# A decoder layer in split float32: three products taken from 256 tokens as columns to 512 weight columns with the tokens on partitions

## The chip, the cores and the metric

One core of one Trainium2 chip runs the whole kernel. The metric is device microseconds of one execution; smaller is better. The kernel before took 768.17 us, the median of three runs (767.91 to 768.85).

## The reference, cut to what matters

One layer on 256 tokens of width 1024, all in float32: a feed-forward block, a mixer with two branches in parallel (a Mamba-2 state-space branch, "SSD", of inner width 2048, and a differential attention of 8 heads), and a second feed-forward block. The part around the change is this:

```
u = rmsnorm(h, mix_pre_g)
z, xbc, dt_raw, q, k, v, gate_logits = split(u @ w_in)          # gate_logits: 2 x 1024 columns
y_ssd = ssd_branch(...)     # ends in  y (256 x 2048) @ ssd_w_branch (2048 x 1024)
y_att = diff_attn_branch(...)   # ends in  o (256 x 1024) @ da_w_branch (1024 x 1024)
gates = sigmoid(gate_logits + gate_b).reshape(b, L, 2, D_MODEL)
merged = gates[:, :, 0] * y_ssd + gates[:, :, 1] * y_att
h = h + rmsnorm(merged @ w_out, mix_post_g)
```

In the attention each head has two score matrices; its weights are softmax(first) minus lambda times softmax(second), causal, with a linear position bias, and the output of each head is normalised over its 128 columns before da_w_branch.

## The kernel before, in words

**Three terms for each product.** TensorE is fed with fp32r, a rounded float32. So each operand is split in two, a high part (the rounded value) and a low part (what is left), and a product is the sum of three: high by high, low by high and high by low. Activations are split by `split` (L185), a cast on ScalarE (L186) and a subtraction on VectorE (L187); weights likewise when they have been loaded (L162 and L163).

**Weights.** They come in chunks of 1 MB, in the order in which they are used, on SP's DMA queue into three buffers (tag `raw`). `take` (L175) hands out the halves of the next chunk and sees to it that the splits of the chunks behind it have been issued, three chunks ahead (AHEAD). The splits, two high and two low tiles of 128 x 1024 for a chunk, and most other larger tiles share 29 buffers of 4 KB in each partition (tag `k4`).

**Two kinds of product.** `mm_t` (L189) makes a transposed result: the weight's 128 columns are the stationary operand, and the 256 tokens are the moving columns, so channels lie on partitions. A chunk of 1024 rows by 256 columns makes 2 blocks of 128 channels with 8 x 3 matmuls each, 48 in all. `mm_nat` (L218) makes a natural result: 128 tokens are the stationary operand, and 512 columns of weights move, so tokens lie on partitions. A chunk there is 512 rows by 512 columns and makes, for each of two blocks of tokens, 4 x 3 matmuls, 24 in all. Before the change, `mm_nat` makes only the V product and the first products of the feed-forward blocks (its matmul is L227).

**Order of the stages.** Feed-forward 1; the mixer's norm; V; dt, B, C and xs with the convolution; z; q and k; then the gates (8 chunks, L944 to L958, tile `pgt`), the SSD branch's product (8 chunks, L966 to L974, tile `pws`), the attention branch's product (4 chunks, L981 to L992, tile `pwd`), w_out (4 chunks, `mm_n`, L408), and feed-forward 2. `mm_n` takes the merged result with channels on partitions (it is its stationary operand there) and gives tokens on partitions. The gates' bias and the sigmoid are applied with channels on partitions: ScalarE adds the bias, one column for each 128 channels from a table of constants, as it empties PSUM. The two branches' results are multiplied by the gates on VectorE, in place in the gates' tiles, and the merged tile is split for w_out.

**Background work.** What lies between the large products is written as generators that are put in a queue and run piece by piece between the chunks: the products inside the SSD branch (`ssd_work`), its norm (`ssd_norm`), and the attention (`att_work`, L821). After each chunk `back.run(BG_US)` issues pieces worth 2.8 us of estimated time. A head of the attention issues: scores (PE, tile `psc`), mask and position bias (DVE), the maximum (DVE), four exponentials with their sums (ACT), the weighting by the sums and the difference (DVE), three transposes (PE, tile `pa`), a copy (ACT, tile `aT`) and two value products (PE, tile `po`). After every second head comes the norm of the pair: a square on ACT, a sum over partitions as a product with ones (PE, tile `pno`), a logarithm and an exponential (ACT), a multiplication (DVE) and a split. ScalarE's tables of functions are loaded explicitly (L234): one for exponentials and logarithms, one for the sigmoid, one for SiLU. Before the SSD branch's product, pieces are run until its input is there; after it, all that is left of the attention.

**The order on each engine.** In the first part of the program and in the tail of `mm_n` it is the order written (`own_order`). From the end of the mixer's first products on it is chosen by the scheduler of the language when the kernel is built (`free_order`), each engine having one queue that is worked in order.

**PSUM.** Three banks rotate for the large products (`pj`), five for everything else (`bg`). A bank has 512 float32 in each partition. In `mm_t` one bank holds both blocks of 128 channels.

Of the kernel before, what the change touches and what calls it, by code (L numbers as in the profile page):

```python
# [15 lines left out]
F32R = mybir.dt.float32r  # L16
AF = mybir.ActivationFunctionType
ALU = mybir.AluOpType
# [6 lines left out]
P = 128  # L25
T = 256
D = 1024
FF = 2816
KD = D // P
# [12 lines left out]
BG_US = 2.8  # L42
# [3 lines left out]
def tile_hybrid_layer(ctx: ExitStack, tc: tile.TileContext, x, ffn1_pre_g, ffn1_w_gate, ffn1_w_up,  # L46
# [4 lines left out]
    nc = tc.nc  # L51
# [5 lines left out]
    def k4(shape, name, dt=F32):  # L57
        return sb.tile(shape, dt, tag="k4", name=name, bufs=K4_BUFS)
# [13 lines left out]
    def pj(name):  # L72

        return ps.tile([P, 512], F32, tag="pj", name=name, bufs=3)

    def pjt(name):

        return pj(name).rearrange("p (m t) -> p m t", m=2)

    def bg(shape, name):  # L80
        return ps.tile(shape, F32, tag="bg", name=name, bufs=5)
# [4 lines left out]
    def t_chunk(w, k0, c0):  # L86
        chunks.append((w[k0:k0 + D, c0:c0 + T].rearrange("(j p) c -> p j c", p=P), [P, KD, T]))

    def s_chunk(w, k0, c0):
        chunks.append((w[k0:k0 + 512, c0:c0 + 512].rearrange("(j p) c -> p j c", p=P), [P, 4, 512]))  # L90
# [4 lines left out]
    w_in2 = w_in[0]  # L95
    Z0, XS0, B0, C0, DT0, Q0, KK0, V0, G0 = 0, 2048, 4096, 4608, 5120, 5152, 6176, 7200, 8224
# [21 lines left out]
    for c in range(4):  # L118
        t_chunk(w_in2, 0, Q0 + c * T)
        t_chunk(w_in2, 0, KK0 + c * T)  # L120
    for c in range(8):
        t_chunk(w_in2, 0, G0 + c * T)
    for c in range(4):
        t_chunk(ssd_w_branch[0], 0, c * T)
        t_chunk(ssd_w_branch[0], D, c * T)
    for c in range(4):
        t_chunk(da_w_branch[0], 0, c * T)
    for c in range(4):
        n_chunk(w_out[0], c * 2 * P)
    ffn_chunks(ffn2_w_gate, ffn2_w_up, ffn2_w_down)  # L130
# [38 lines left out]
    def split_to(n):  # L169

        while len(splits) < min(n, len(chunks)):
            for _ in split_steps():
                pass

    def take(ahead=AHEAD):  # L175

        i = taken[0]
        taken[0] += 1
        split_to(i + ahead)
        his, los = splits[i]  # L180
        splits[i] = None
        nj = chunks[i][1][1] // 2
        return (lambda j: his[j // nj][:, j % nj, :], lambda j: los[j // nj][:, j % nj, :])

    def split(hi, lo, src):  # L185
        nc.scalar.copy(hi, src)  # L186
        nc.vector.tensor_sub(lo, src, hi.bitcast(F32))  # L187

    def mm_t(acc, w, act, k0=0, first=True, last=True):  # L189

        (wh, wl), (ah, al, _) = w, act
        acc = acc if isinstance(acc, list) else [acc[:, m, :] for m in range(2)]
        for m in range(2):
            cs = slice(m * P, (m + 1) * P)
            for j in range(KD):
                nc.tensor.matmul(acc[m], wh(j)[:, cs], ah(k0 + j), start=first and j == 0, stop=False)  # L196
                nc.tensor.matmul(acc[m], wh(j)[:, cs], al(k0 + j), start=False, stop=False)  # L197
            for j in range(KD):
                nc.tensor.matmul(acc[m], wl(j)[:, cs], ah(k0 + j), start=False,  # L199
                                 stop=last and j == KD - 1)  # L200
# [17 lines left out]
    def mm_nat(acc, w, act, k0, first, last, late):  # L218


        (wh, wl), (ah, al) = w, act
        pairs = [(ah, wh), (al, wh), (ah, wl)] if late == "w" else [(ah, wh), (ah, wl), (al, wh)]
        terms = [(p, j) for j in range(4) for p in pairs[:2]] if late == "w" else \
            [(p, j) for p in pairs[:2] for j in range(4)]
        terms += [(pairs[2], j) for j in range(4)]
        for i, ((a, b), j) in enumerate(terms):
            nc.tensor.matmul(acc, a(k0 + j), b(j), start=first and i == 0, stop=last and i == 11)  # L227
# [5 lines left out]
    def act_table(name):  # L233
        f = nc.scalar.preload_act_table_set(name)  # L234
        for prev in act_since:
            tc.add_manual_dep(f.ins, prev, order, reason="activation table")
        act_since.clear()
        act_fence[0] = f.ins.name

    def act(*args, **kw):  # L240
        a = nc.scalar.activation(*args, **kw)
        if act_fence[0] is not None:
            tc.add_manual_dep(a.ins, act_fence[0], order, reason="activation table")
        act_since.append(a.ins.name)
# [19 lines left out]
    halves = (slice(0, 512), slice(512, D))  # L264
# [8 lines left out]
    ident = const.tile([P, P], F32, name="ident")  # L273
# [19 lines left out]
    pt = bg([P, KD], "pt_cols_f")  # L293
    nc.tensor.transpose(pt, stage_f, ident[:KD, :KD])
    nc.vector.tensor_copy(cols_f, pt)
    cols_a = const.tile([P, P], F32, name="cols_a")
    col, gain_rows = {}, []
    row = 0
    for name, v in (("mx", mix_pre_g), ("f2", ffn2_pre_g), ("gb", gate_b),
                    ("ng", ssd_norm_g), ("cb", ssd_conv_b), ("sg", da_subln_g)):  # L300
        n = v.shape[1] // P
        gain_rows.append((row, n, v))
        col[name] = row
        row += n
# [4 lines left out]
    def new_u(tag):  # L309
        for i in range(2):  # L310
            uT[i] = sb.tile([P, 4, 2, T], F32R, tag="u8", name=f"u{i}_{tag}", bufs=2)

    act_u = (lambda j: uT[j // 4][:, j % 4, 0, :], lambda j: uT[j // 4][:, j % 4, 1, :],
             lambda j: uT[j // 4][:, j % 4, :, :])
    uh, ul, _ = act_u
# [87 lines left out]
    def load_gain(v, name):  # L403
        pg = k4([P, D], name)
        nc.gpsimd.dma_start(pg, v[0].partition_broadcast(P))
        return pg
# [197 lines left out]
    pt = bg([P, P], "pt_cols_b")  # L604
# [13 lines left out]
    for o, n, off in ((0, P, 0), (P, T, P)):  # L618
        v = dneg[:, o:o + n]
# [110 lines left out]
    for i in range(4):  # L730
        acc = pjt(f"pbc{i}")
# [17 lines left out]
    yh = [None] * 4  # L749
    yl = [None] * 4  # L750
# [67 lines left out]
    oh = [None] * 2  # L818
    ol = [None] * 2
# [85 lines left out]
    back = Background()  # L905
    back.add(cb_work())
    for g in range(4):
        xs[g] = k4([P, 4, T], f"xs{g}")
        for i in range(2):
            acc = pjt(f"pxs{g}{i}")  # L910
# [5 lines left out]
    for g in range(4):  # L916
        sz[g] = k4([P, 4, T], f"sz{g}")
        for i in range(2):
            acc = pjt(f"pz{g}{i}")
# [8 lines left out]
    for c in range(4):  # L928
# [4 lines left out]
        acc = pjt(f"pq{c}")  # L933
# [3 lines left out]
        acc = pjt(f"pk{c}")  # L937
# [3 lines left out]

    back.add(att_work())

    def gates(half):  # L944
        tiles = []
        for c in range(4):
            if c % 2 == 0:
                tiles.append(k4([P, 4, T], f"gt{half}{c}"))
            acc = pjt(f"pgt{half}{c}")
            mm_t(acc, take(), act_u)  # L950
            for m in range(2):
                n = col["gb"] + half * 8 + c * 2 + m
                nc.scalar.activation(tiles[-1][:, (c % 2) * 2 + m, :], acc[:, m, :], AF.Identity,
                                     bias=cols_a[:, n:n + 1])
            back.run(BG_US)
        return tiles

    gt0, gt1 = gates(0), gates(1)  # L958
    act_table(SIGMOID)
    for t in gt0 + gt1:  # L960
        act(t, t, AF.Sigmoid)
    act_table(EXP_LN)
    while yl[3] is None:
        back.run(0.1)
    act_y = (lambda j: yh[j // 4][:, j % 4, :], lambda j: yl[j // 4][:, j % 4, :], None)
    for c in range(4):  # L966
        acc = [pj(f"pws{c}{m}")[:, :T] for m in range(2)]
        mm_t(acc, take(), act_y, 0, True, False)
        back.run(BG_US)
        mm_t(acc, take(), act_y, KD, False, True)  # L970
        for m in range(2):
            t = gt0[c // 2][:, (c % 2) * 2 + m, :]
            nc.vector.tensor_tensor(t, acc[m], t, ALU.mult)
        back.run(BG_US)  # L974
    del act_y
    yh = yl = None
    back.drain()
    act_table(SILU)
    act_o = (lambda j: oh[j // 4][:, j % 4, :], lambda j: ol[j // 4][:, j % 4, :], None)
    mg = []  # L980
    for c in range(4):  # L981
        acc = pjt(f"pwd{c}")
        mm_t(acc, take(), act_o)
        cs = slice((c % 2) * 2, (c % 2) * 2 + 2)
        t0, t1 = gt0[c // 2][:, cs, :], gt1[c // 2][:, cs, :]
        nc.vector.tensor_tensor(t1, acc, t1, ALU.mult)
        nc.vector.tensor_tensor(t1, t1, t0, ALU.add)
        if c % 2 == 0:
            mh = k4([P, 4, T], f"mh{c}", F32R)
            ml = k4([P, 4, T], f"ml{c}", F32R)  # L990
        split(mh[:, cs, :], ml[:, cs, :], t1)
        mg += [(mh[:, cs.start + m, :], ml[:, cs.start + m, :]) for m in range(2)]  # L992
    pg = load_gain(mix_post_g, "pg_mx")
    acc = [[bg([P, 512], f"acc_mx{b}{q}") for q in range(2)] for b in range(2)]

# [49 lines left out]
```

## Time and the profile before

| | us |
|---|---|
| three runs | 767.91, 768.17, 768.85 |
| profiled execution | 768.8 |
| its span | 766.0 |
| PE busy in it | 751.8 (98%) |
| DVE busy | 522.5 (68%) |
| ACT busy | 441.7 (58%) |
| POOL busy | 32.7 (4%) |
| gates, from first product to the first of the SSD branch | 411.70 to 468.70 |
| SSD branch | 468.70 to 529.00 |
| attention branch | 529.00 to 552.05 |
| w_out | 552.05 to 574.74 |
| feed-forward 2 to the end | 574.74 to 766.0 |

PE is TensorE's queue of matmuls, PEld its loads of stationary operands, DVE VectorE, ACT ScalarE, POOL GpSimd and SP the engine that issues most DMAs. In the timeline, a row gives the start and the duration in us, the engine, the line of the kernel, the operation with out<-in tiles, partitions x elements, and how many like it follow each other; in brackets stands the idle time of the engine before it with what ended it. In a table by stretches, the columns are the stretch, its length, busy time and number of instructions of PE, PEld, DVE, ACT and POOL, the granted clock of TensorE, the DMA engines' busy share, and GB/s. In a group of instructions the columns after the bar are busy time in us and mean duration in ns. Matmuls follow each other before the last has ended, so their durations overlap.

### The profile page before, as it was taken

What the parts mean: (1) busy time and instruction counts of PE and PEld (TensorE: products, weight loads), DVE (VectorE), ACT (ScalarE), POOL (GpSimd) and SP (SyncE); (2) the same over time, 40 slices, a digit from 0 to 9 for tenths busy, and PEclk for the clock granted to TensorE, in tenths of its full rate; (3) what the DMA queues carried; (4) which work ended last, traced back from release to release, by engine and by line L of the source; (5) the groups of instructions that cost most, each with busy time, mean ns of one, the idle gap of its engine ahead of it and who ended that gap; (6) DMA issues with size and microseconds to landing.
All of it is one profiled execution on the core that took longest, in us unless ns stands there. A gap on an engine that the chain in (4) does not pass through costs nothing.

```text
span 766.0 us, 11904 instructions
## 1 busy us (share of the span) xinstructions
PE 751.8 (98%) x4811; PEld 668.9 (87%) x4811; DVE 522.5 (68%) x815; ACT 441.7 (58%) x721; POOL 32.7 (4%) x73
## 2 busy tenths in 40 slices
PE   8899999999999999999999999999999999999996
PEld 6688888888889999899999988989988888888885
DVE  5586677654577888887868777676785767666612
ACT  7475566553566565666836767665573656555511
POOL 3300000000200000000000000000011000000000
PEclk9999999999999999999999999999999999999999
DMA  9576665586253638465535554436481676545801
GB/s 322 131 237 204 220 220 219 172 297 219 62 165 113 214 119 267 145 219 177 182 110 172 160 164 143 133 114 217 171 296 56 200 240 194 173 169 186 296 0 55
DMA packets 104199, 136.97 MB, mean 179 GB/s; under 512 B 2668, under 2 KB 88784, under 8 KB 104144
## 3 DMA queue, kind: packets, MB, share of 16 engines
q1 hardware_dynamic: 101728, 129.51, 51.4%
q0 software_dynamic: 2112, 6.18, 2.6%
q8 instruction: 37, 0.61, 0.3%
q10 hardware_dynamic: 304, 0.53, 0.2%
q14 instruction: 18, 0.15, 0.1%
HBM read 135.13 MB, written 1.08 MB: 178 GB/s over the span
## 4 chain that ended last, share of the span: by engine, by line
PE 88%; DVE 4%; ACT 3%; issue 1%; POOL 0%; DVEq 0%; POOLq 0%; ACTq 0%
PE acc_f L422 16%; PE pup_f L212 9%; PE pg_f L212 9%; PE pn_f L227 4%; PE pg_f L211 4%; PE pup_f L211 4%; PE pn_mx L227 3%; PE acc_mx L422 3%; PE pxs L197 2%; PE pxs L199 2%; PE pxs L196 2%; PE pz L196 2%; PE pz L199 2%; PE pz L197 2%; PE pgt L199 1%; PE pgt L196 1%
## 5 line engine op out<-in xcount | busy, mean ns | idle before, releaser
L163 DVE TENSOR_TENSOR wlo<-raw,whi 128x1024 fp32r<-128x1024 f32 (+1 forms) x246 | 291.2, 1211 | 47.5 <-ACT whi L162 47.1
L162 ACT CAST whi<-raw 128x1024 fp32r<-128x1024 f32 (+1 forms) x246 | 247.1, 1042 | 52.8 <-PE acc_f L422 18.4
L212 PE MATMUL pg_f<-u_f,whi 128*128 128x512 f32 x288 | 101.2, 396 | 0.0
L212 PE MATMUL pup_f<-u_f,whi 128*128 128x512 f32 x288 | 101.1, 396 | 0.0
L211 PE MATMUL pg_f<-u_f,wlo 128*128 128x256 f32 x252 | 70.6, 280 | 0.0
L211 PE MATMUL pup_f<-u_f,wlo 128*128 128x256 f32 x252 | 70.4, 279 | 0.0
L212 PEld LDWEIGHTS pg_f<-u_f,whi 128*128 128x128 f32 x288 | 53.0, 188 | 9.6
L212 PEld LDWEIGHTS pup_f<-u_f,whi 128*128 128x128 f32 x288 | 52.8, 188 | 9.7
L422 PE MATMUL acc_f<-whi,gh_f 128*128 128x512 f32 x176 | 58.2, 390 | 0.0
L422 PE MATMUL acc_f<-wlo,gh_f 128*128 128x512 f32 x176 | 58.2, 390 | 0.0
L422 PE MATMUL acc_f<-whi,gl_f 128*128 128x512 f32 x176 | 58.1, 389 | 0.0
L211 PEld LDWEIGHTS pup_f<-u_f,wlo 128*128 128x128 f32 x252 | 47.6, 189 | 1.6
L211 PEld LDWEIGHTS pg_f<-u_f,wlo 128*128 128x128 f32 x252 | 47.6, 189 | 1.6
L216 DVE TENSOR_TENSOR su_f<-pup_f,su_f 128x256 f32<-128x256 f32 x36 | 15.2, 421 | 39.7 <-ACT su_f L215 39.7
L422 PEld LDWEIGHTS acc_f<-wlo,gh_f 128*128 128x128 f32 x176 | 33.0, 188 | 6.9
L422 PEld LDWEIGHTS acc_f<-whi,gl_f 128*128 128x128 f32 x176 | 33.0, 188 | 6.8
L422 PEld LDWEIGHTS acc_f<-whi,gh_f 128*128 128x128 f32 x176 | 33.1, 188 | 6.7
L197 PE MATMUL pws<-yl,whi 128*128 128x256 f32 x128 | 32.8, 291 | 0.0
L196 PE MATMUL pz<-u_mx,whi 128*128 128x256 f32 x128 | 32.3, 289 | 0.0
L196 PE MATMUL pgt<-u_mx,whi 128*128 128x256 f32 x128 | 32.2, 288 | 0.0
L196 PE MATMUL pws<-yh,whi 128*128 128x256 f32 x128 | 32.0, 285 | 0.0
L197 PE MATMUL pgt<-u_mx,whi 128*128 128x256 f32 x128 | 31.8, 284 | 0.0
(305 smaller groups left out, 1574.1 us busy)
## 6 DMA issues: line engine op xcount, KB each, us to landing
raw<-in_w_in_dram SPq DMA_DIRECT2D x40, 1024.0 KB, 5.5
raw<-in_ffn_w_down_dram SPq DMA_DIRECT2D x22, 1024.0 KB, 5.0
raw<-in_ffn_w_gate_dram SPq DMA_DIRECT2D x20, 1024.0 KB, 5.9
raw<-in_ffn_w_up_dram SPq DMA_DIRECT2D x20, 1024.0 KB, 5.7
raw<-in_ssd_w_branch_dram SPq DMA_DIRECT2D x8, 1024.0 KB, 5.3
acb<-acd POOLq DMA_DIRECT2D x8, 512.0 KB, 4.0
raw<-in_da_w_branch_dram SPq DMA_DIRECT2D x4, 1024.0 KB, 5.3
raw<-in_w_out_dram SPq DMA_DIRECT2D x4, 1024.0 KB, 6.2
```

Source lines behind the costliest of these rows:

```text
L162: nc.scalar.copy(hi[:, js, :], r[:, q * nj + j:q * nj + j + n, :])
L163: nc.vector.tensor_sub(lo[:, js, :], r[:, q * nj + j:q * nj + j + n, :], hi[:, js, :].bitcast(F32))
L196: nc.tensor.matmul(acc[m], wh(j)[:, cs], ah(k0 + j), start=first and j == 0, stop=False)
L197: nc.tensor.matmul(acc[m], wh(j)[:, cs], al(k0 + j), start=False, stop=False)
L199: nc.tensor.matmul(acc[m], wl(j)[:, cs], ah(k0 + j), start=False, stop=last and j == KD - 1)
L211: nc.tensor.matmul(acc[:, :T], wl(j)[:, cs], ah(j), start=False, stop=False)
L212: nc.tensor.matmul(acc, wh(j)[:, cs], ahl(j), start=j == 0, stop=j == KD - 1)
L216: nc.vector.tensor_tensor(dst[:, m, :], acc[:, :T], dst[:, m, :], ALU.add)
L227: nc.tensor.matmul(acc, a(k0 + j), b(j), start=first and i == 0, stop=last and i == 11)
L422: nc.tensor.matmul(acc[b][q], x_[:, ts], w_(kt)[:, halves[q]], start=i == 0 and kt == 0 and x_ is ah and w_ is wh, stop=i == n - 1 and kt ...
```

## The change

The gates, the SSD branch and the attention branch are made with `mm_nat` instead of `mm_t`: each chunk is 512 rows by 512 columns, and the result has tokens on partitions. A helper, `natural`, keeps two PSUM banks (one for each block of 128 tokens), runs over the n chunks that make up 512 result columns (2 for the gates and the attention branch, 4 for the SSD branch), hands each finished bank to a function that empties it, and runs the background after each chunk (after those of the attention branch with nothing).

- The gates' bias lies along the free dimension now, so it isn't a column of the table of constants any more (16 rows fewer): it is loaded on POOL's queue as two broadcasts over all partitions into two k4 tiles, and VectorE adds it as it empties PSUM, in two pieces of 512 columns for each tile.
- The tiles of the gates are now by half (first or second branch) and block of tokens, 1024 columns each: four tiles as before.
- The merge is made for each block of tokens and 512 columns: VectorE multiplies and adds, TensorE transposes the four squares of 128 x 128 into a `bg` bank, and ScalarE and VectorE split from there, for w_out, which is as before.

The number of chunks (20), their order among the stages, and the bytes of weights stay the same.

```diff
-    for c in range(8):
-        t_chunk(w_in2, 0, G0 + c * T)
     for c in range(4):
-        t_chunk(ssd_w_branch[0], 0, c * T)
-        t_chunk(ssd_w_branch[0], D, c * T)
-    for c in range(4):
-        t_chunk(da_w_branch[0], 0, c * T)
+        for k0 in (0, 512):
+            s_chunk(w_in2, k0, G0 + c * 512)
+    for c in range(2):
+        for k0 in range(0, 2 * D, 512):
+            s_chunk(ssd_w_branch[0], k0, c * 512)
+    for c in range(2):
+        for k0 in (0, 512):
+            s_chunk(da_w_branch[0], k0, c * 512)
...
-    for name, v in (("mx", mix_pre_g), ("f2", ffn2_pre_g), ("gb", gate_b),
+    for name, v in (("mx", mix_pre_g), ("f2", ffn2_pre_g),
...
-    def gates(half):
...
-    gt0, gt1 = gates(0), gates(1)
+    def natural(name, n, hi, lo, evict, us):
+        accs = [pj(f"{name}{b}") for b in range(2)]
+        for i in range(n):
+            w = take()
+            for b in range(2):
+                bs = slice(b * P, (b + 1) * P)
+                mm_nat(accs[b], w, (lambda k: hi(k)[:, bs], lambda k: lo(k)[:, bs]), i * 4, i == 0, i == n - 1, "u")
+                if i == n - 1:
+                    evict(b, accs[b])
+            back.run(us)
+
+    gt = [[None] * 2 for _ in range(2)]
+    for half in range(2):
+        gb = k4([P, D], f"gb{half}")
+        nc.gpsimd.dma_start(gb, gate_b[0][half * D:(half + 1) * D].partition_broadcast(P))
+        for b in range(2):
+            gt[half][b] = k4([P, D], f"gt{half}{b}")
+        for q in range(2):
+            def gate(b, acc):
+                nc.vector.tensor_tensor(gt[half][b][:, halves[q]], acc, gb[:, halves[q]], ALU.add)
+            natural(f"pgt{half}{q}", 2, uh, ul, gate, BG_US)
     act_table(SIGMOID)
-    for t in gt0 + gt1:
+    for t in gt[0] + gt[1]:
         act(t, t, AF.Sigmoid)
     act_table(EXP_LN)
     while yl[3] is None:
         back.run(0.1)
...
-    for c in range(4):
-        acc = [pj(f"pws{c}{m}")[:, :T] for m in range(2)]
-        mm_t(acc, take(), act_y, 0, True, False)
-        back.run(BG_US)
-        mm_t(acc, take(), act_y, KD, False, True)
-        for m in range(2):
-            t = gt0[c // 2][:, (c % 2) * 2 + m, :]
-            nc.vector.tensor_tensor(t, acc[m], t, ALU.mult)
-        back.run(BG_US)
+    for q in range(2):
+        def gated(b, acc):
+            t = gt[0][b][:, halves[q]]
+            nc.vector.tensor_tensor(t, acc, t, ALU.mult)
+        natural(f"pws{q}", 4, lambda j: yh[j // 4][:, j % 4, :], lambda j: yl[j // 4][:, j % 4, :], gated, BG_US)
     yh = yl = None
     back.drain()
     act_table(SILU)
     mg = []
-    for c in range(4):
-        acc = pjt(f"pwd{c}")
-        mm_t(acc, take(), act_o)
...
-        nc.vector.tensor_tensor(t1, acc, t1, ALU.mult)
-        nc.vector.tensor_tensor(t1, t1, t0, ALU.add)
...
-        split(mh[:, cs, :], ml[:, cs, :], t1)
+    for q in range(2):
+        mh = k4([P, 4, T], f"mh{q}", F32R)
+        ml = k4([P, 4, T], f"ml{q}", F32R)
+        mg += [(mh[:, m, :], ml[:, m, :]) for m in range(4)]
+        def merge(b, acc):
+            t0, t1 = gt[0][b][:, halves[q]], gt[1][b][:, halves[q]]
+            nc.vector.tensor_tensor(t1, acc, t1, ALU.mult)
+            nc.vector.tensor_tensor(t1, t1, t0, ALU.add)
+            pt = bg([P, 4, P], f"pmg{q}{b}")
+            for m in range(4):
+                nc.tensor.transpose(pt[:, m, :], t1[:, m * P:(m + 1) * P], ident)
+            bs = slice(b * P, (b + 1) * P)
+            split(mh[:, :, bs], ml[:, :, bs], pt)
+        natural(f"pwd{q}", 2, lambda j: oh[j // 4][:, j % 4, :], lambda j: ol[j // 4][:, j % 4, :], merge, 0.0)
```

More of the change, by code (lines that the diff above doesn't have):

```diff
@@ L942, in tile_hybrid_layer @@
     back.add(att_work())
-    def gates(half):
-        tiles = []
-        for c in range(4):
[L947 to L950, printed above, removed]
-            for m in range(2):
-                n = col["gb"] + half * 8 + c * 2 + m
-                nc.scalar.activation(tiles[-1][:, (c % 2) * 2 + m, :], acc[:, m, :], AF.Identity,
-                                     bias=cols_a[:, n:n + 1])
-            back.run(BG_US)
-        return tiles
-    gt0, gt1 = gates(0), gates(1)
+    def natural(name, n, hi, lo, evict, us):
[18 more added lines that the diff above has]
+            natural(f"pgt{half}{q}", 2, uh, ul, gate, BG_US)
     act_table(SIGMOID)
-    for t in gt0 + gt1:
+    for t in gt[0] + gt[1]:
         act(t, t, AF.Sigmoid)
@@ L964, in tile_hybrid_layer @@
         back.run(0.1)
-    act_y = (lambda j: yh[j // 4][:, j % 4, :], lambda j: yl[j // 4][:, j % 4, :], None)
-    for c in range(4):
-        acc = [pj(f"pws{c}{m}")[:, :T] for m in range(2)]
-        mm_t(acc, take(), act_y, 0, True, False)
-        back.run(BG_US)
-        mm_t(acc, take(), act_y, KD, False, True)
-        for m in range(2):
-            t = gt0[c // 2][:, (c % 2) * 2 + m, :]
-            nc.vector.tensor_tensor(t, acc[m], t, ALU.mult)
-        back.run(BG_US)
-    del act_y
+    for q in range(2):
[3 more added lines that the diff above has]
+        natural(f"pws{q}", 4, lambda j: yh[j // 4][:, j % 4, :], lambda j: yl[j // 4][:, j % 4, :], gated, BG_US)
     yh = yl = None
@@ L978, in tile_hybrid_layer @@
     act_table(SILU)
-    act_o = (lambda j: oh[j // 4][:, j % 4, :], lambda j: ol[j // 4][:, j % 4, :], None)
     mg = []
-    for c in range(4):
-        acc = pjt(f"pwd{c}")
-        mm_t(acc, take(), act_o)
[L984 to L990, printed above, removed]
-        split(mh[:, cs, :], ml[:, cs, :], t1)
-        mg += [(mh[:, cs.start + m, :], ml[:, cs.start + m, :]) for m in range(2)]
+    for q in range(2):
[12 more added lines that the diff above has]
+        natural(f"pwd{q}", 2, lambda j: oh[j // 4][:, j % 4, :], lambda j: ol[j // 4][:, j % 4, :], merge, 0.0)
     pg = load_gain(mix_post_g, "pg_mx")
```

## The prediction

> **What bounds the kernel now.** The page first, then the busy time cut at the first and last instruction of the three products in question.
>
> ```profile
> span 766.0 us, 11904 instructions
> PE 88%; DVE 4%; ACT 3%; issue 1%; POOL 0%; DVEq 0%; POOLq 0%; ACTq 0%
> 411.70:552.05 140.35, 138.47 (x1095) 129.71 (x1094) 100.24 (x163) 92.84 (x168) 0.53 (x1) 1.00 0.46 155
> ```
>
> The chain that ended last is 88% TensorE (PE). The gates, the SSD branch and the attention branch take from 411.70 to 552.05, 140.35 us, at granted clock 1.00, with DVE busy 100, ACT 93 and a DMA share of 0.46: PE sets the time and the loads don't. The built orders of the two kernels agree on PE up to the first gate product, and the change touches nothing behind the w_out product but what it delays. So the sum is made inside these 140.35 us.
>
> The trap is in the mean durations:
>
> ```profile
> L196 PE MATMUL pgt<-u_mx,whi 128*128 128x256 f32 x128 | 32.2, 288 | 0.0
> L422 PE MATMUL acc_f<-whi,gh_f 128*128 128x512 f32 x176 | 58.2, 390 | 0.0
> ```
>
> Two of 288 ns against one of 390 would promise 186 ns for each pair, some 90 us. But matmuls overlap; what counts is from start to start. The attention branch alone fills a window with its 192 matmuls; the 512-column products of the same helper (mm_nat) stand in the timeline:
>
> ```profile
> 529.00:552.05 23.05, 23.05 (x195) 23.05 (x194) 13.56 (x17) 9.10 (x11) 0.53 (x1) 1.00 0.39 146
> 576.55 1.98 PE L227 MATMUL pn_f<-whi,u_f 128*128 128x512 f32 x8
> 578.37 1.07 PE L227 MATMUL pn_f<-wlo,u_f 128*128 128x512 f32 x4
> 579.27 1.98 PE L227 MATMUL pn_f<-whi,u_f 128*128 128x512 f32 x8
> ```
>
> 23.05 / 192 = 0.120 us for 256 columns; (579.27 - 576.55) / 12 = 0.2267 us for 512.
>
> **Products.** Before, 8 + 8 + 4 chunks at 48 matmuls: 960 x 0.120 = 115.2 us. After, 24 for each chunk: 480 x 0.2267 = 108.8. **-6.3 us**. (The Trainium skill, "TensorE: Matmul & The Clock Gate", section Back-to-back issue gap, gives N/2.4 + 2.5 ns for the isolated gap, which is 109.2 and 215.8 ns here and would leave only an estimated 1.2 us of gain. The trace has 120 and 227; it decides.)
>
> **Transposes.** 16 of 128x128, in four groups of 4. Such a group before:
>
> ```profile
> 594.94 0.60 PE L517 MATMUL pt_f<-ident,sg_f2b 128*128 128x128 f32 x4
> 595.30 1.18 PE L227 MATMUL pn_f<-whi,u_f 128*128 128x512 f32 x4
> ```
>
> 0.36 us each group: **+1.4 us**.
>
> **The softmax chain of the background.** 115.2 of the 140.35 us are products; the other 25 are the attention heads, put between them piece by piece, and the waits. Each head is a chain over three engines: scores (PE), mask, maximum (DVE), exponentials (ACT), weighting (DVE), transposes (PE), copy (ACT), values (PE). It is hidden as long as PE has products between its own pieces. In the middle of the SSD branch it is barely hidden now:
>
> ```profile
> 477.44 0.69 ACT L241 ACTIVATE sqo<-pno,eps_c 128x512 f32<-128x512 f32 x1 [0.29 <-PE pno L871]
> ...
> 478.81 1.28 ACT L234 ACT_TABLE_LOAD   x1
> 480.63 3.90 ACT L241 ACTIVATE gt<-gt 128x1024 f32<-128x1024 f32 x4
> 484.53 1.28 ACT L234 ACT_TABLE_LOAD   x1
> 489.02 0.30 PE L860 MATMUL pa<-ident,s 128*128 128x128 f32 x1 [0.61 <-DVE s L855]
> 489.81 0.48 ACT L863 COPY aT<-pa 128x384 f32<-128x384 f32 x1 [0.24 <-PE pa L860]
> 494.43 0.40 ACT L241 ACTIVATE s<-s,nm 128x128 f32<-128x128 f32 x1 [4.13 <-DVE nm L839]
> ...
> 499.91 0.60 ACT L869 ACTIVATE sqo<-po 128x512 f32<-128x512 f32 x1 [1.01 <-PE po L867]
> 501.73 0.69 ACT L241 ACTIVATE sqo<-pno,eps_c 128x512 f32<-128x512 f32 x1 [1.22 <-PE pno L871]
> ...
> 504.42 1.05 ACT L162 CAST whi<-raw 128x1024 fp32r<-128x1024 f32 x1
> ```
>
> From the second pair's norm (477.44) over two table loads, the sigmoids and two whole heads to the cast of the sixth SSD chunk's weights (done 505.47) are 28.0 us, and each step starts within 0.3 us of what it needs: work of PE delays it nowhere by more than that. PE's cover meanwhile:
>
> ```profile
> L197 PE MATMUL pws<-yl,whi 128*128 128x256 f32 x58 | 14.6, 288 | 0.0
> L196 PE MATMUL pws<-yh,whi 128*128 128x256 f32 x58 | 14.5, 286 | 0.0
> L199 PE MATMUL pws<-yh,wlo 128*128 128x256 f32 x56 | 8.4, 287 | 0.0
> 476.27 1.13 PE L871 MATMUL pno<-sqo,ones 128*128 128x512 f32 x2
> 477.33 0.50 PE L833 MATMUL psc<-k,q 64*128 64x128 f32 x4
> 478.19 0.39 PE L196 MATMUL pws<-yh,whi 128*128 128x256 f32 x1
> 490.68 0.60 PE L866 MATMUL po<-aT,v 128*128 128x256 f32 x2
> 491.43 0.50 PE L833 MATMUL psc<-k,q 64*128 64x128 f32 x4
> 498.00 0.38 PE L860 MATMUL pa<-ident,s 128*128 128x128 f32 x2
> 498.14 0.84 PE L199 MATMUL pws<-yh,wlo 128*128 128x256 f32 x5
> ```
>
> The first three rows are grouped over 478.19 to 505.46: 172 products, 20.6 us. The others give one head's pieces by their starts: norm 1.06, scores 0.86, values 0.75, transposes about 0.2; the stretch holds two heads' worth and one norm, 4.7 us. 27.3 - 20.6 - 4.7 = 2.0 us lost.
>
> In the changed kernel's built order ACT's order in this stretch is the same, but that the casts of the fifth chunk come before it and not within: the sixth chunk's cast still stands behind the third pair's norm. PE's order isn't the same. Relative to the chunks the heads stand one chunk later, and between that norm and the sixth chunk PE has only 18 + 24 + 24 products, 66 x 0.2267 = 15.0 us; with three sets of scores, two of transposes and values and a norm (2.6 + 0.4 + 1.5 + 1.1) 20.5. The chain is 28.0. PE stands 7.5 us, against 2.0: **+5.5 us**. Most of it lies in one place: behind the scores of the sixth head PE has 18 products (4.1 us), and then transposes, values, norm and scores follow each other with nothing between them.
>
> The other six heads: the second head's scores end at 445.00 and its transposes start at 450.76:
>
> ```profile
> 445.00 0.85 PE L199 MATMUL pgt<-u_mx,wlo 128*128 128x256 f32 x5
> 450.76 0.30 PE L860 MATMUL pa<-ident,s 128*128 128x128 f32 x1
> ```
>
> 5.8 us, of which 0.4 are a cast that the new order has elsewhere. After, 21 products (4.8 us) cover it: 0.6 to 0.8 us of wait. Counting products in the same way gives 0.3 to 1.2 for the others, and once some 0.5 for a gate bank that DVE empties late. I take 0.75 each, 4.5, against about 1.5 lost there before: **+3.0 us** (bounds -1.5, no wait at all, and +6).
>
> **The merge.** Before, the merge ends in a split on ACT and DVE beside PE. Now transposes stand in PE's queue and wait for DVE:
>
> ```profile
> 534.97 0.69 DVE L986 TENSOR_TENSOR gt<-pwd,gt 128x512 f32<-128x512 f32 x1 [5.33 <-PE pwd L199]
> 535.69 0.69 DVE L987 TENSOR_TENSOR gt<-gt,gt 128x512 f32<-128x512 f32 x1
> L163 DVE TENSOR_TENSOR wlo<-raw,whi 128x1024 fp32r<-128x1024 f32 x43 | 51.0, 1220 | 2.0 <-ACT whi L162 1.9
> ```
>
> 0.69 + 0.69 and about 0.3 of signals is 1.7 us. The built order puts 7, 12, 7 and 0 products between the block that ends and its transposes: 1.6 us of cover in the first and third (0.1 each), 2.7 in the second, where a weight split (1.22) stands between multiply and add (0.2), and none in the last, which has such a split too: 1.7 + 1.2 = 2.9. Everything of w_out is queued behind it. **+3.2 us** (bounds 1.7 and 5).
>
> **At nothing:** the gates' eviction moves from ACT to DVE, eight adds of 0.69 us; DVE is busy 100 of 140 us, and three PSUM banks for two accumulators leave a block of 12 products (2.7 us) to do it; uncovered it would be 5.5. The bias comes as two broadcasts on POOL's queue:
>
> ```profile
> pg_mx<-in_mix_post_g_dram POOLq DMA_DIRECT2D x1, 512.0 KB, 5.6
> ```
>
> By the built order the second is issued six products before the first gate half ends and first used a chunk and a half later, over 8 us for 5.6; in POOL's queue only the w_out gain stands behind it. Uncovered: 6 us. SP's order of loads is unchanged. The constant's 16 rows go for nothing.
>
> **Sum:** -6.3 + 1.4 + 5.5 + 3.0 + 3.2 = **+6.8 us**. The profiled execution took 768.8 (span 766.0 and 2.8 around it): 775.6. The median of the runs lies 0.6 lower: **775.0 us**.
>
> **Rivals.** *Faster, the chain stays covered* (12%): DVE and ACT reach the heads sooner than I count, PE loses in the softmax stretches no more than now, and the last merge has its add ahead of the split: -6.3 + 1.4 + 1.7 = -3.2, 765 us. It decides if PE's wait in the 28 us stays at 2.0. For it: the wait view gives PE under 2 us in the stage now. Against: every ACT row above starts on its input, and ACT's order is kept. Half-way cases, within 0.2%, 10%.
>
> *Weights late* (9%): two bias tiles join the 29 shared buffers, and by the built order the casts of most gate and SSD chunks wait for products two chunks before. A split is 2 x 1.04 on ACT and a last 1.22 on DVE; queued behind a softmax it would eat the chunk of slack (5.4 us), about 1 us for each of 8 chunks: 783 us.
>
> *The clock drops* (8%):
>
> ```profile
> 760.00:762.00 2.00, 0.00 (x0) 0.00 (x0) 1.47 (x3) 0.14 (x2) 0.86 (x2) 1.00 0.00 0
> 762.00:764.00 2.00, 0.00 (x0) 0.00 (x0) 0.63 (x1) 0.00 (x0) 0.00 (x0) 1.00 0.58 218
> 764.00:766.00 2.00, 0.00 (x0) 0.00 (x0) 0.00 (x0) 0.00 (x0) 0.00 (x0) 0.65 0.12 44
> ```
>
> After the last product the clock holds 1.00 for over 4 us of idleness, then falls. The new hole has 2.9 us of small pieces spread over 9 us, its longest gap about 3. If the clock falls there, the pieces double (+2.9) and some 4 us of products behind run at half (+2): 780 us. (The Trainium skill, same page, section Why this matters for your kernels, puts the limit at gaps of about 3 us. By that rule this happens; the trace's 4 us at 1.00 speak against.)
>
> *The products gain nothing* (3%): 0.240 a pair for 512 columns as well, +6.3: 781 us. The rows of the same helper speak against it.
>
> **Chances.** Forecast 58%, 771 to 779. About 0.2% (1.5 us) is what a measurement of this kernel can tell from no change. Faster by more: 0.12, the first rival. Within: 0.12, the half-way cases and the forecast's edge. Slower: 0.76. The range, 767 to 782, leaves out the first rival's middle and the weights-late case; it takes in the half-way cases, the clock, and the head and merge bounds.
>
> **What would show it.** Product spacing 0.227; on PE a wait of about 6 us around the sixth head, ended by the cast of the sixth SSD chunk, and one of about 3 us ahead of the last merge transposes; ACT's 28 us stretch unchanged; first gate product still at 411.7; 147 us from there to w_out. I am wrong if the stretch is much shorter, or if PE waits for casts in the gates.

## The result, and the profile after

The changed kernel takes 775.69 us (median of five runs, 772.97 to 776.09), the kernel before 767.91: a ratio of 1.0093 (95% interval 1.0079 to 1.0107), 0.9% slower. The forecast was 775.0. The sum behind it holds less well than its total: two of its terms were wrong, in opposite directions.

The profiled run is the shortest of the five, 772.97 us with a span of 771.3. From the page and the table by stretches (gates, SSD branch, attention branch, the rest):

```profile
span 771.3 us, 10971 instructions
PE 750.2 (97%) x4347; PEld 643.4 (83%) x4347; DVE 526.0 (68%) x819; ACT 435.5 (56%) x705; POOL 32.4 (4%) x74
411.28:463.47 52.19, 51.59 (x239) 40.07 (x237) 40.90 (x66) 30.74 (x56) 0.53 (x1) 1.00 0.50 165
463.47:530.21 66.74, 60.71 (x282) 45.54 (x280) 48.11 (x85) 45.87 (x85) 0.00 (x0) 0.97 0.45 156
530.21:557.10 26.89, 24.19 (x113) 19.18 (x112) 17.44 (x22) 11.53 (x14) 0.53 (x1) 1.00 0.50 181
557.10:771.30 214.20, 207.46 (x1061) 175.88 (x1059) 128.03 (x172) 105.29 (x169) 6.86 (x14) 0.99 0.48 165
```

The three stages take 145.82 us instead of 140.35, 5.5 more: 57.00 to 52.19 in the gates, 60.30 to 66.74 in the SSD branch, 23.05 to 26.89 in the attention branch. What lies behind them has hardly moved (213.95 to 214.20). PE has less to do and waits more; its waits in the three stages, by what ended them, are in us in total, how often, and the longest:

```profile
PE pws L229 <- ACT whi L164: 3.0, 1, 3.0
PE pmg L998 <- DVE gt L995: 2.7, 1, 2.7
PE pa L862 <- DVE s L857: 2.1, 4, 1.0
PE pno L873 <- ACT sqo L871: 0.7, 1, 0.7
PE po L868 <- ACT aT L865: 0.6, 1, 0.6
PE pgt L229 <- DVE gt L968: 0.2, 1, 0.2
```

9.3 us, against 1.8 in the same view of the kernel before:

```profile
PE pa L860 <- DVE s L855: 1.6, 4, 0.6
PE pn L801 <- DVE sqy L799: 0.2, 1, 0.2
```

Most of it belongs to one place. The timeline there, ACT first and then PE:

```profile
480.52 0.69 ACT L243 ACTIVATE sqo<-pno,eps_c 128x512 f32<-128x512 f32 x1 [1.22 <-PE pno L873]
...
483.71 3.90 ACT L243 ACTIVATE gt<-gt 128x1024 f32<-128x1024 f32 x4
...
497.28 0.40 ACT L243 ACTIVATE s<-s,nm 128x128 f32<-128x128 f32 x1 [3.90 <-DVE nm L841]
...
507.25 1.04 ACT L164 CAST whi<-raw 128x1024 fp32r<-128x1024 f32 x1
...
498.45 1.07 PE L229 MATMUL pws<-whi,yl 128*128 128x512 f32 x4
500.48 0.74 PE L862 MATMUL pa<-ident,s 128*128 128x128 f32 x3 [0.96 <-DVE s L857]
501.79 0.70 PE L868 MATMUL po<-aT,v 128*128 128x256 f32 x2 [0.57 <-ACT aT L865]
...
503.40 1.12 PE L873 MATMUL pno<-sqo,ones 128*128 128x512 f32 x2 [0.69 <-ACT sqo L871]
...
504.78 0.61 PE L836 MATMUL psc<-k,q 64*128 64x256 f32 x4
508.35 2.93 PE L229 MATMUL pws<-whi,yh 128*128 128x512 f32 x6 [2.96 <-ACT whi L164]
...
556.72 0.63 PE L998 MATMUL pmg<-ident,gt 128*128 128x128 f32 x4 [2.67 <-DVE gt L995]
```

From the second pair's norm (480.52) to the end of the sixth SSD chunk's cast (508.29) the chain takes 27.8 us, against 28.0 before; on PE it is 27.9 from the scores behind that norm (480.41) to that chunk's first product (508.35). PE runs out of products at 499.5, does the sixth head's last pieces one after the other with a wait ahead of each, and then stands until the cast. The last row is the merge.

The last products but one hold something that the sum did not have: six products take 2.93 us where six of 0.2267 would take 1.5. The granted clock, by the microsecond (the third number from the end of a row):

```profile
507.00:508.00 1.00, 0.00 (x0) 0.00 (x0) 0.97 (x2) 1.00 (x2) 0.00 (x0) 0.90 0.00 0
508.00:509.00 1.00, 0.66 (x2) 0.56 (x3) 1.00 (x4) 1.00 (x4) 0.00 (x0) 0.50 0.00 0
...
510.00:511.00 1.00, 1.00 (x3) 0.79 (x3) 1.00 (x1) 1.00 (x7) 0.00 (x0) 0.50 0.00 0
511.00:512.00 1.00, 1.00 (x5) 0.79 (x4) 0.96 (x6) 1.00 (x3) 0.00 (x0) 0.89 0.00 0
```

From 507.8 to 511.2 it stands at half. The eight products from 508.35 to 511.60 take 3.25 us instead of 1.81: 1.4 us lost.

### The profile page after: what moved, and what is told of

Its sections match the earlier page's. It is cut to its first block, busy times and chain, and to the rows that moved or that the text cites. A ratio compares the mean times of both kernels' runs of the same rounds, so it can differ in the third digit from the quotient of the medians.

```text
span 771.3 us, 10971 instructions
## 1 busy us (share of the span) xinstructions
PE 750.2 (97%) x4347; PEld 643.4 (83%) x4347; DVE 526.0 (68%) x819; ACT 435.5 (56%) x705; POOL 32.4 (4%) x74
## 4 chain that ended last, share of the span: by engine, by line
PE 88%; DVE 4%; ACT 3%; issue 1%; POOL 0%; DVEq 0%; POOLq 0%; ACTq 0%
PE acc_f L424 16%; PE pup_f L214 9%; PE pg_f L214 9%; PE pgt L229 4%; PE pn_f L229 4%; PE pg_f L213 4%; PE pup_f L213 4%; PE pws L229 3%; PE pn_mx L229 3%; PE acc_mx L424 3%; PE pwd L229 3%; PE pxs L201 2%; PE pxs L199 2%; PE pxs L198 2%; PE pz L198 2%; PE pz L201 2%
## 5 line engine op out<-in xcount | busy, mean ns | idle before, releaser
L229 PE MATMUL pgt<-whi,u_mx 128*128 128x512 f32 x128 | 33.9, 398 | 0.2 <-DVE gt L968 0.2
L198 PE MATMUL pz<-u_mx,whi 128*128 128x256 f32 x128 | 32.3, 288 | 0.0
L199 PE MATMUL pz<-u_mx,whi 128*128 128x256 f32 x128 | 31.7, 284 | 0.0
L198 PE MATMUL pxs<-u_mx,whi 128*128 128x256 f32 x128 | 31.7, 285 | 0.0
L199 PE MATMUL pxs<-u_mx,whi 128*128 128x256 f32 x128 | 31.4, 283 | 0.0
```

## The experiments

All were measured beside the kernel before on the same chip (767.8 to 768.3 us).

**The changed kernel again, for a second profile.** No edit.

> The changed kernel once more, unaltered, for a second profile: the one at hand is the shortest of its five runs (772.97 us, mean clock 0.995), the others took 775.5 to 776.1 at 0.990 or 0.991. If the clock falls behind the holes alone, a profile of about 775.7 us shows the same waits and the same stretch lengths in everything but the half-speed stretches: a longer one in the SSD branch, or a second one behind the merge, some 9 us at 0.50 in place of 3.2. If something else differs, the waits do.

776.51 us (ratio 1.0113, 1.0097 to 1.0130), the profiled run 776.48. The waits of PE are the same (2.9, 2.7, 2.1, 0.7, 0.6 and 0.2). The clock isn't; the SSD branch in steps of 2 us, and one row from behind the merge:

```profile
504.00:506.00 2.00, 2.00 (x8) 0.83 (x8) 0.00 (x0) 0.69 (x1) 0.00 (x0) 0.50 0.00 0
...
508.00:510.00 2.00, 0.27 (x1) 0.27 (x2) 1.97 (x4) 1.89 (x5) 0.00 (x0) 1.00 0.00 0
...
512.00:514.00 2.00, 2.00 (x6) 1.52 (x5) 1.97 (x8) 2.00 (x4) 0.00 (x0) 0.50 0.10 15
...
560.00:561.00 1.00, 1.00 (x4) 0.81 (x3) 1.00 (x2) 1.00 (x2) 0.00 (x0) 0.50 0.29 47
```

Three half-speed stretches in place of one: two in the SSD branch, one ahead of the long wait and one behind it, and a third at the first w_out products. The span is 774.8 us, 3.5 more, with the same waits. So the clock's part of the loss is 1.4 us in the shortest run and about 5 in one of 776.5.

**Without the heads.** `att_work` gives away a split of q in place of the heads' output; the same edit in both kernels.

```diff
-                s = k3([P, 2, 3 * P], f"s{hd}")
...
-            split(oh[hp // 2][:, o:o + 2, :], ol[hp // 2][:, o:o + 2, :], sq)
+            split(oh[hp // 2][:, o:o + 2, :], ol[hp // 2][:, o:o + 2, :], qT[hp // 2][:, o:o + 2, :])
```

> The kernel before with the attention heads left out: q is split and given to da_w_branch in place of the heads' output; all else stays. It shows the products by themselves. 960 products of 256 columns at 0.120 us are 115.2 us, so the stretch from the first gate product to w_out takes about 116 us instead of 140.35, and the run 744 us.

> The changed kernel with the heads left out in the same way. My account: 480 x 0.2267 = 108.8, transposes 1.4, the last merge's wait 2.9, and perhaps 1.8 for the clock behind it: 113 to 115 us for the stretch, so 1 to 3 us under the kernel before without heads, which is the other sign than with them. Rival, the new form is dearer by itself (gate bias on VectorE, PSUM banks, weights later): 118 us or more, slower than the other without heads too.

The kernel before takes 744.02 us so, the changed one 743.60. The three stretches of the one and of the other:

```profile
411.40:459.00 47.60, 47.40 (x391) 46.95 (x390) 33.60 (x38) 37.31 (x52) 0.00 (x0) 1.00 0.57 180
459.00:505.10 46.10, 46.10 (x387) 46.10 (x386) 23.26 (x24) 19.23 (x21) 0.00 (x0) 1.00 0.62 212
505.10:528.10 23.00, 23.00 (x194) 23.00 (x193) 13.52 (x17) 9.05 (x11) 0.53 (x1) 1.00 0.39 147
```

```profile
411.00:456.00 45.00, 44.92 (x199) 36.71 (x198) 36.37 (x44) 31.18 (x37) 0.53 (x1) 1.00 0.65 213
456.00:499.50 43.50, 43.50 (x194) 36.02 (x193) 26.63 (x24) 21.30 (x22) 0.00 (x0) 1.00 0.66 225
499.50:526.50 27.00, 24.42 (x114) 19.54 (x112) 14.44 (x19) 8.39 (x10) 0.53 (x1) 0.99 0.40 142
```

Gates and SSD branch are 2.6 us shorter each, 5.2 together; counted were 768 x 0.120 - 384 x 0.2267 = 5.1. The attention branch is 4.0 longer. In all 116.7 against 115.5 us: slightly in favour of the change, 1.2 us, at the lower edge of what I expected (the 115.5 lie half a microsecond above my range for it). The runs differ by only 0.4 us, since the clock falls behind the changed one's merge (525.8 to 529.2), at the cost of w_out's first products. Without the heads nothing is left of the 5.5 us, so the new form as a whole isn't dearer by itself. Taken from 140.35 and 145.82, the heads cost 23.7 us in the kernel before and 30.3 in the changed one.

**The hole filled.** Twelve products that nobody reads, with a dependency that puts them behind the seventh head's scores on PE.

```diff
+                if hd == 6:
+                    filler = bg([P, 512], "filler")
+                    for fi in range(12):
+                        f = nc.tensor.matmul(filler, yh[0][:, 0, :P], yh[0][:, 0:2, :].rearrange("p a b -> p (a b)"),
+                                             start=True, stop=True)
+                        tc.add_manual_dep(f.ins, last.ins.name, order, reason="filler")
                 yield 0.9
```

> The changed kernel, with 12 products of 512 columns that nobody reads, put on PE's queue behind the seventh head's scores, where the hole of about 3.4 us lies (504.95 to 508.35); the order of all else on PE is the same. At 0.2267 us they take 2.7 us. My account: the hole is time in which PE has nothing to do while the chain runs on ACT and DVE, so the work costs nothing, and with PE never idle for so long the clock stays at 1.00: 1.6 us less, 774.0 us, in spite of more work. Rival 1, the clock fall has another cause: 775.7, half speed at the same place. Rival 2, PE is the bound there: 778.4.

773.40 us (ratio 1.0065, 1.0053 to 1.0077): 2.3 to 3.1 us less than the changed kernel's two medians, with more work. On PE:

```profile
503.20 1.13 PE L879 MATMUL pno<-sqo,ones 128*128 128x512 f32 x2 [0.69 <-ACT sqo L877]
...
504.58 0.61 PE L836 MATMUL psc<-k,q 64*128 64x256 f32 x4
505.12 3.03 PE L841 MATMUL filler<-yh 128*128 128x512 f32 x12
508.16 2.06 PE L229 MATMUL pws<-whi,yh 128*128 128x512 f32 x6
```

The next product starts at 508.16, as it did at 508.35 behind an empty PE, and the six now take 2.06 us instead of 2.93. The hole was idle time, and the idleness slowed what came behind it. In this profile the clock falls at the merge's wait instead (555.5 to 558.9), so this run has one half-speed stretch like the changed kernel's shortest, and about its time (773.54 against 772.97 us).

**Heads lapped.** The scores and the mask of a head go ahead of the weighting of the one before; in the changed kernel and in the kernel before.

```diff
     def att_work():
+        s_next = scores(0)
+        yield 0.9
...
-                s = k3([P, 2, 3 * P], f"s{hd}")
...
+                s = s_next
...
                 yield 1.0
+                if hd < 7:
+                    s_next = scores(hd + 1)
+                    yield 0.9
                 nc.vector.reciprocal(sm, sm)
```

> The changed kernel, with the scores and the mask of the next attention head issued before the weighting and the transposes of the present one; no work added or taken away. My account: what costs time is the softmax chain over three engines, too long for the products that PE has beside it. The step takes scores, mask and part of the signals (0.86 + 1.0 + some 0.5 us) off the chain for each head, so the 27.9 us from the second pair's norm to the sixth SSD chunk's cast fall to about 21, and the hole of 3.0 us, the half-speed stretch behind it (3.2 us at clock 0.50, 1.6 us lost) and most of the waits for the weighting (2.1 us) go: 768 to 770 us. Rival: PE waits for weights whose cast ACT does late in any case: the hole stays, 775.7.

> The same step made in the kernel before, by itself. My account: there PE loses only 2.0 us in the middle of the SSD branch and about 1.5 us around the other heads, so no more than 3.5 us are to be had: 765 to 767 us. Rival, that heads are hidden in the kernel before and only the new form brings the chain to light: 768.0, no change. If the gain were as large as in the changed kernel, the chain would cost both kernels the same and could not be the cause of the difference.

The changed kernel falls to 765.67 us (ratio to the kernel before 0.9967, 0.9956 to 0.9979), some 10 us; the kernel before to 767.23 (0.9985, 0.9976 to 0.9994), about 1. All waits of PE that are left in the changed one, and its SSD branch:

```profile
PE pmg L1005 <- DVE gt L1002: 2.7, 1, 2.7
PE pa L869 <- DVE s L864: 0.2, 1, 0.2
```

```profile
466.10:522.10 56.00, 55.85 (x259) 42.32 (x258) 45.07 (x74) 43.18 (x76) 0.00 (x0) 1.00 0.55 183
```

No wait for the softmax but 0.2 us; granted clock 1.00. Gates and SSD branch together take 110.8 us (411.30 to 522.10) instead of 118.9: 8.1 less, of which 1.4 is the clock. The whole run gains more than that and more than I expected; that a typical run is saved two half-speed stretches of the SSD branch, as in the second profile, and not only the one of the first, would explain it. One reserve: with the pieces in another order, the scheduler also puts the sigmoids ahead of the second pair's norm (467.27 instead of 483.71), and lays the heads' pieces otherwise between the products, so the step is more than a shorter chain.

**Without the sigmoids.** A second way to shorten the chain, again in both.

```diff
-    act_table(SIGMOID)
-    for t in gt[0] + gt[1]:
-        act(t, t, AF.Sigmoid)
-    act_table(EXP_LN)
```

> The changed kernel with the four sigmoids and the two table loads around them left out (the gates are used without sigmoid): 3.9 + 2 x 1.28 = 6.5 us less on ACT, in the middle of the 27.9 us chain, and no less work for PE. My account: the chain falls to 21.4 us, beside which PE has 20.5 us of work, so the hole and the half-speed stretch behind it go, and what is left is the merge's wait: gates and SSD branch together 111 to 113 us instead of 118.9, the run 768 to 770 us. Rival: the hole has its cause in the order that the scheduler gives PE, or in the weights: 774 us or more.

> The kernel before with the same left out. My account: its chain of 28.0 us had 26 us of work of PE beside it, so no more than 2.0 us are to be had, though the same 6.5 us leave ACT: 765.5 to 767 us. Rival: ACT's work counts by itself, and both kernels gain the same.

The changed kernel takes 769.03 us, about 7 less; the kernel before 768.60 (ratio 1.0011, 1.0001 to 1.0020), if anything more. In the changed one:

```profile
PE pmg L994 <- DVE gt L991: 2.7, 1, 2.7
PE pws L229 <- ACT whi L164: 1.4, 1, 1.4
PE pa L862 <- DVE s L857: 1.0, 3, 0.4
PE pgt L229 <- DVE gt L968: 0.2, 1, 0.2
```

The wait for the cast falls from 3.0 to 1.4 us; it doesn't go, since the chain only falls from 27.8 to 23.6 us (on ACT, 479.86 to 503.42): part of the 6.5 us lay beside mask and maximum of the fifth head, which now end last. Gates and SSD branch take 113.9 us, not the 111 to 113 that I expected. For the kernel before I expected up to 2.0 us of gain and there is none: with 6.5 us less on ACT the scheduler changes PE's order too, and its SSD branch even takes 61.1 us instead of 60.3. That both gain the same is refuted all the same.

**The last transposes behind w_out's first chunk.**

```diff
-            pt = bg([P, 4, P], f"pmg{q}{b}")
...
+            def turn_back():
+                pt = bg([P, 4, P], f"pmg{q}{b}")
...
+            if (q, b) == (1, 1):
+                last_turn.append(turn_back)
+            else:
+                turn_back()
...
                 one(i, w, ((0, (0, 1)), (1, (0, 1))))
+                if first_done is not None:
+                    first_done()
```

> The changed kernel, with the last of the four groups of merge transposes (and its split) issued behind the 24 products of w_out's first chunk, which need only the first half of the merged result. My account: PE's wait of 2.67 us ahead of those transposes is gone and nothing takes its place, because 24 x 0.2267 = 5.4 us of products lie over the 2.9 us of multiply, split and add. The time falls by 2.7 us, to 773.0 us; if the four slower runs of the changed kernel (775.5 to 776.1, mean clock 0.990 against 0.995 in the profiled 773.0) lose their clock behind this hole, by up to 5.4, to 770.3. Rival: the merge was never what w_out waited for (its weights or a bank would be late next): 775.7 and a wait of the same size at the first w_out product.

770.83 us (ratio 1.0044, 1.0027 to 1.0060), five less than the changed kernel; four runs lie between 769.7 and 771.0, the others at 773.4 and 774.0. The profiled one is of the latter, and shows why:

```profile
500.00:502.00 2.00, 0.99 (x4) 0.59 (x5) 0.69 (x3) 0.48 (x1) 0.00 (x0) 1.00 0.00 0
502.00:504.00 2.00, 1.31 (x5) 0.90 (x5) 0.00 (x0) 0.60 (x1) 0.00 (x0) 0.52 0.00 0
...
508.00:510.00 2.00, 0.00 (x0) 0.00 (x0) 1.97 (x4) 1.29 (x2) 0.00 (x0) 0.50 0.00 0
...
514.00:516.00 2.00, 2.00 (x7) 1.57 (x6) 2.00 (x4) 0.87 (x1) 0.00 (x0) 0.56 0.82 226
```

Here the clock falls at 502.1, before the long wait, and stays at half to 515.8, nearly 14 us. The merge's wait is gone in it, and no fall stands behind the merge.

**Both steps.**

> The changed kernel with both steps, heads lapped and the last merge transposes behind w_out's first chunk. My account: after the first step alone (765.67 us) the one long wait of PE left in these stages is that of 2.67 us ahead of the last transposes, with a half-speed stretch of about 4 us behind it (548.6 to 552.9, some 1.8 us lost). Both go: 761 us, 0.9% under the kernel before. Rival: without the wait, w_out's weights or the norm behind it are what is late, so that the two steps don't add up: 764 us or more.

761.67 us: a ratio of 0.9919 to the kernel before (0.9904 to 0.9934). It beats both kernels, and the kernel before with lapped heads too: 0.7%, some 5 us, by their ratios to the kernel before (0.9919 against 0.9985; the two were measured on different chips). Around the merge, PE goes from the last product of the attention branch to w_out without a wait, and the transposes come 5.5 us later:

```profile
544.14 1.08 PE L229 MATMUL pwd<-whi,ol 128*128 128x512 f32 x4
545.07 0.63 PE L424 MATMUL acc_mx<-whi,mh 128*128 128x512 f32 x2
...
550.54 0.60 PE L1009 MATMUL pmg<-ident,gt 128*128 128x128 f32 x4
```

Its three stretches take 54.8, 56.0 and 23.6 us, 134.4 in all, at clock 1.00; the last transposes now lie behind them, in w_out. (The half-speed stretch that was to go lasts 3.4 us by the shares of its rows, 548.7 to 552.2, and not the 4 that I expected.)

## Why the prediction was right, point by point

- **Products, -6.3: right.** A block of four starts every 0.907 us where nothing disturbs it, 0.2267 each; without the heads, gates and SSD branch are shorter by 5.2 us (counted 5.1). The isolated gap of the Trainium skill ("TensorE: Matmul & The Clock Gate", section Back-to-back issue gap), which left only an estimated 1.2 us, isn't the spacing here: 120 and 226.7 ns stand against its 109.2 and 215.8.
- **The softmax chain of the middle, +5.5: right, in its place, size and cause.** In PE's 27.9 us lie 66 products and the pieces of two heads and more (20.5 us), so 7.4 us are lost where 7.5 were counted, 2.0 before: +5.4. That it is idle time is shown by the filled hole; that it is the chain, by the two ways of shortening it, each of which gains the changed kernel 7 to 10 us and the kernel before at most 1. One thing stays open: the last and longest wait is for a cast that stands behind the chain in ACT's queue, and no run moves that cast alone. ACT was idle for 3.90 us ahead of 497.28, and whether the cast could have gone there, with its buffers free, wasn't tried; so the length of the chain and the place of the cast behind it aren't separated.
- **The other six heads, +3.0: wrong.** I allowed each 0.75 us of wait. Outside the bad stretch the view of waits has 0.28 and 0.30 us for the weighting and 0.25 for a gate bank, 0.8 us in all for six heads, no more than in the kernel before. Gates and SSD branch together are 1.6 us longer; -5.1 for products, +5.4 for the hole and +1.4 for the clock make 1.7, and leave nothing for these heads. To count the products between two pieces says how much cover there is, but not that it is too little; only where the chain is longer than it does PE wait.
- **The merge, +1.4 and +3.2: right, a little low.** The attention branch is 3.84 us longer; with 1.3 us saved on products and 1.4 for transposes that leaves 3.7. The wait ahead of the last transposes is 2.8 of it, from start to start (2.67 in the view), with the weight split (1.21) between multiply and add, as the built order had it. The other 0.9 lies around the first three groups, 0.2 to 0.3 us at each more than the 0.36 counted, where the view shows no wait; 0.4 were counted. (The parts of the forecast's 3.2 add up to 3.3.)
- **At nothing: right.** The gates' addition on VectorE costs PE 0.2 us; the broadcasts landed in 4.4 and 7.4 us, and no wait for them shows.
- **The clock: a rival at 8% that came true.** I let the row of the tail decide, over 4 us of idleness at clock 1.00. But the clock fell at the hole in all three profiles that have it in full, and the price was 1.4 us in the shortest run and about 5 in the other. I also had it in one place only; behind the merge's wait of 2.6 to 2.7 us it fell in four of the six profiles that have that wait. The limit of gaps of about 3 us in the Trainium skill (the same page, section Why this matters for your kernels), which I had set against the tail's row, was the better guide, and is itself a little high for these.

In the profiled run: -6.4 + 1.4 + 5.4 + 0 + 3.7 + 1.4 = 5.5 us, against a forecast of 6.8. (The stretch begins 0.4 us earlier, what follows is 0.25 longer, and 1.7 us instead of 2.8 lie around the span: 773.0.) The typical run adds some 3 us of slower clock. So the products, the chain and the merge were right for their reasons, but that the total came within a microsecond is luck: the 3.0 us for the other heads, which aren't there, stood in for the clock, which was put at nothing.

## What to carry to other kernels

When a change takes work off the busiest engine, look first at what that work was hiding: here 6 us less of products beside an unchanged chain of 28 us over three engines became 5.4 us of waiting in one spot. Compare the length of such a chain with the work that the built order puts beside it, stretch by stretch, and don't add a fee for each piece that is covered. A hole in TensorE's queue can cost more than its length (here a wait of 2.96 us was followed by 1.4 us lost to half speed), so fill it with work that is ready (the next head's scores, the next product's first chunk): with the holes closed, the same change is worth 0.7% (761.67 us, a ratio of 0.9919, against 767.23, 0.9985, of the kernel before with lapped heads) instead of costing 0.9%.

## What the runs showed of the hardware

The half-speed stretches ahead of the last product, their ends worked out from the shares in rows like those above, have one length: 507.8 to 511.2 in the changed kernel, 3.4 us in each of those behind a merge, 503.9 to 507.3 and 510.7 to 514.1 in the second profile, and 13.7 us, four times that, in one run. A fall doesn't need an idle stretch of that length: it came after 2.6 us of idleness, and twice (502.1 and 503.9) among the small pieces of the sixth head, ahead of which no gap was over 1 us. The Trainium skill, "TensorE: Matmul & The Clock Gate", section Part 1: The HAM clock gate, tells of a window of about 3.4 us that runs freely, not started by the kernel; the lengths agree with it.

So do the places. In the second profile the clock falls at 503.87, 510.70, 558.48 and, behind the last product, 770.11: 2, 14 and 62 steps of 3.413 us from one to the next. Such steps, counted in the first profile from its fall at 507.80, end at 555.6 and cut the merge's wait (554.05 to 556.72) into pieces of 1.5 and 1.1 us; in the second, the one step from 555.07 to 558.48 holds nearly all of it (555.95 to 558.62). That fits one and the same wait of 2.67 us being followed by a fall in the second profile and not in the first. It fits the tail of the kernel before too, on which the prediction relied: the last product ends at 759.36 and the clock falls at 764.59, at the end of the first step without any product.

How busy a step must be for the clock to stay, the runs tell only roughly. In the twelve profiles, counted in this way from the gates on, every step at full speed with PE busy for up to 42% was followed by half speed. Of the nine between 46 and 64%, seven were followed by full speed and two by half (56 and 59%: those with the small pieces of the sixth head in the two runs where it fell there). So the busy share alone doesn't decide there, and no run shows what does.
